# Half-width gated pairs: the norm's factor of the up branch is applied behind the lower projection, and VectorE takes the gate product in PSUM

## The chip, the cores and the metric

The kernel runs on one core of a Trainium2 chip. TensorE (PE) does the matrix products; a product needs a weight load (PEld) and a pass of the moving operand, and writes an accumulator bank of PSUM. VectorE (DVE), ScalarE (ACT) and GpSimd (POOL) do elementwise work; DVE and ACT read and write PSUM and SBUF, while the program uses GpSimd on SBUF tiles alone. Transfers from DRAM are issued by SyncE (SP). Each engine works through its own queue in order; engines wait for one another on semaphores. The metric is the device time of one execution in microseconds, the median of several.

## The reference, cut to what matters

Two layers over 512 tokens of 1024 channels, in float32. Layer 0 is a causal convolution module and a gated feed-forward network; layer 1 is windowed attention and another feed-forward network. The parts that the change touches are the first feed-forward network and its norm:

```python
def rmsnorm(x, g):
    xf = x * lax.rsqrt(jnp.mean(x * x, axis=-1, keepdims=True) + EPS)
    return xf * g

def swiglu_ffn(x, w_up, w_down):
    gate, up = jnp.split(x @ w_up, 2, axis=-1)
    return (jax.nn.silu(gate) * up) @ w_down

h = h + swiglu_ffn(rmsnorm(h, norm_ffn[l]), ffn_w_up[l], ffn_w_down[l])
```

The hidden width is 2816. The norm's factor, rsqrt of the mean square, is one number per token. It passes through a product with a weight matrix, so gate and up can be computed from the unscaled activations and scaled afterwards. In the up branch, which enters linearly, it can also pass through the lower projection; in the gate branch it cannot, because silu is not linear.

## The kernel before, in words

**Layout.** Channels lie on the 128 partitions, tokens along the free dimension. The stream `h` is 8 tiles of 128 channels by 512 tokens. A float32 product is made of three products in a faster format: each operand is split into a rounded part and a rest (`hi`, `lo`), and `mm3` (L254 to L256) adds hi*hi, hi*lo and lo*hi into one bank.

**Weights.** They come as 200-odd chunks of 128 x 1024 in the order of a list (`PLAN`). SyncE loads them up to six chunks ahead (L186). Up to two chunks ahead, ACT casts a chunk to its rounded part (L202, tile `whi`) and DVE subtracts it for the rest (L203, tile `wlo`). Three buffers of each exist, so the cast of a chunk waits until TensorE is done with the chunk three before it.

**Stages.** The convolution's input projection and the first token half's convolution come first. Then, for the first token half (256 tokens): the convolution's output projection (`pw2`, L694) and six of the eleven column pairs of the first feed-forward network (`ffn_part(0, 0, ..)`). The second token half's convolution runs as background work beside that, its steps handed out as TensorE uses up weight chunks. After it `pw2` and the same six pairs for the second token half follow, then the other five pairs for all 512 tokens at once, then layer 1.

**The convolution beside it.** Of the 31 taps of a channel tile, 18 (8 in the first two tiles) go over ACT, which scales a shifted row (L576), and GpSimd, which adds it up (L577). The others are taken by DVE with a multiply and add in PSUM (L584). At the end GpSimd adds both sums (L587); in the first four tiles DVE adds a shift (L611); ACT squares the row (L613); and TensorE sums row and square over channels (L622).

**A half-width pair.** A pair is 256 gate columns and 256 up columns. TensorE makes them in two banks, one for gate and one for up, out of four weight chunks of 24 matmuls each (`ffn_up`). `evac` then works on whole banks (128 x 512, two column tiles by 256 tokens): DVE multiplies gate by the norm's factor into a temporary (L433), ACT takes silu of it (L436), DVE multiplies up by the factor into another temporary (L433 again), GpSimd multiplies both (L437), and `split` makes the rounded part on ACT (L371) and the rest on DVE (L372), the tiles `quad` that the lower projection reads. The first pair's evac is held back until the second pair's second chunk, because the norm's factor is not known earlier.

**The lower projection.** `ffn_part` runs it in two groups of 512 output channels (`down_group`), each with two banks of two output tiles. Behind each group DVE adds the four tiles to `h`, one 128 x 256 tile at a time (L418).

**What orders the work.** The program is built with a scheduler that lays the instructions of each queue in the order of a simulated timeline (`schedule_with_timeline_sim=True`); the order is fixed then. PSUM is a pool of eight banks, and a tile takes whichever slot is free in that timeline. In the background the convolution holds up to four of them. The full-width pairs (512 tokens) have their own branch of `evac` (L441 to L446) and are not edited.

Of the kernel before, what the change touches and what calls it, by code (L numbers as in the profile page):

```python
# [12 lines left out]
AF = mybir.ActivationFunctionType  # L13
# [4 lines left out]
P = 128  # L18
# [130 lines left out]
def hybrid_trunk(ctx: ExitStack, tc: tile.TileContext, xT, W, prm_in, wdw_in, sinks, relb, onehot, outT):  # L149
    nc = tc.nc  # L150
# [10 lines left out]
    def uid(s):  # L161
        ctr[0] += 1
        return f"{s}{ctr[0]}"

    def bank():
        return ps.tile([P, 512], F32, tag="bank", name=uid("bank"))
# [4 lines left out]
    def temp():  # L171
        return tmp.tile([P, 512], F32, tag="tmp", name=uid("tmp"))

    def f32(ap):
        return ap.bitcast(F32)
# [95 lines left out]
    hT = cpool.tile([P, KT, S], F32, tag="h", name="h")  # L271
# [98 lines left out]
    def split(dst, src):  # L370
        nc.scalar.copy(dst[0], src)  # L371
        nc.vector.tensor_sub(dst[1], src, f32(dst[0]))  # L372

    def cut(pair, tok):
        return pair[0][:, tok], pair[1][:, tok]


    def accs(w):
        if w == 512:
            return [bank() for _ in range(4)]  # L380
        return [b[:, e * w:(e + 1) * w] for b in (bank(), bank()) for e in range(2)]

    def opens(m, w):
        return w == 512 or m % 2 == 0

    def closes(m, w):
        return w == 512 or m % 2 == 1


    def down_group(keys, act_of, banks, on_step=None):  # L390
        nk = len(keys)
        w = banks[0].shape[-1]
        for ci, (key, kts) in enumerate(keys):
            whi, wlo = get(*key)
            order = [(k, m) for k in range(2) for m in range(4)]
            if ci == nk - 1:
                order = [(k, m) for m in range(4) for k in range(2)]
            for k, m in order:
                sl = slice(m * P, (m + 1) * P)
                mm3(banks[m], (whi[:, k, sl], wlo and wlo[:, k, sl]), act_of(kts + k),  # L400
                    ci == 0 and k == 0 and opens(m, w), ci == nk - 1 and k == 1 and closes(m, w))
                if on_step is not None and ci < nk - 1 and m == 3:
                    on_step()
            if on_step is not None and ci == nk - 1:
                on_step()
                on_step()

    def ffn_part(layer, part, xg, tok, rms, on_h=None):
        lo, hi = (HALVES0, HALVES1)[layer][part]
        hid = ffn_up(layer, lo, hi, xg, tok, rms)  # L410
        w = tok.stop - tok.start
        for g in range(2):
            banks = accs(w)
            down_group([(("down", layer, kp, g), 2 * (kp - lo)) for kp in range(lo, hi)],
                       lambda kt: hid[kt], banks)
            for m in range(4):
                t = h[g * 4 + m][:, tok]
                nc.vector.tensor_add(t, banks[m], t)  # L418
                if on_h is not None:
                    on_h(g * 4 + m)  # L420

    def ffn_up(layer, lo, hi, xg, tok, rms):
        w = tok.stop - tok.start
        hid = Act(2 * (hi - lo), w)

        def evac(pair, banks):
            rs_bc = rms.step2()
            if w == 256:
                i = 2 * (pair - lo)
                dst = [q[:, i % 8:i % 8 + 2, :].rearrange("p a s -> p (a s)") for q in hid.q[i // 8]]  # L430
                t1, t2 = temp(), temp()
                for t, b in ((t1, banks[0]), (t2, banks[1])):
                    nc.vector.tensor_mul(t.rearrange("p (a s) -> p a s", a=2), b.rearrange("p (a s) -> p a s", a=2),  # L433
                                         rs_bc.unsqueeze(1).to_broadcast([P, 2, w]))
                    if t is t1:
                        nc.scalar.activation(t, t, AF.Silu)  # L436
                nc.gpsimd.tensor_mul(t2, t1, t2)  # L437
                split(dst, t2)
                return
            for m in range(2):  # L440
                t1, t2 = temp()[:, 0:w], temp()[:, 0:w]  # L441
                nc.vector.tensor_mul(t1, banks[m], rs_bc)  # L442
                nc.scalar.activation(t1, t1, AF.Silu)  # L443
                nc.vector.tensor_mul(t2, banks[2 + m], rs_bc)  # L444
                nc.gpsimd.tensor_mul(t2, t1, t2)  # L445
                split(hid[2 * (pair - lo) + m], t2)  # L446

        pending = []
        for pair in range(lo, hi):
            if w == 256:  # L450
                full = [bank(), bank()]
                banks = [b[:, e * w:(e + 1) * w] for b in full for e in range(2)]
            else:
                full = banks = accs(w)
            for half in range(2):
                for which in range(2):
                    whi, wlo = get("up", layer, pair, half, which)
                    order = [(k, m) for k in range(4) for m in range(2)]
                    if half == 1:
                        order = [(k, m) for m in range(2) for k in range(4)]  # L460
                    for k, m in order:
                        sl = slice(m * P, (m + 1) * P)
                        mm3(banks[which * 2 + m], (whi[:, k, sl], wlo[:, k, sl]), cut(xg[half * 4 + k], tok),
                            half == 0 and k == 0 and opens(m, w), half == 1 and k == 3 and closes(m, w))
                    if half == 0 and which == 1:
                        if w == 512:
                            rms.step1()
                        for p in pending:
                            evac(*p)
                        pending = []  # L470
            if w == 256 and pair == lo:
                rms.step1()
                pending.append((pair, full))
            else:
                evac(pair, full)
        return hid

    class Next:
# [5 lines left out]
        def on_h(self, i):  # L484
            if self.x is None:
                self.x = {self.gains[0]: Act(KT)}
            if self.rms is None:
                self.bc = new_bc() if self.bc is None else self.bc
                self.rms = Rms(self.bc, self.tok)
            g = self.gains[0]  # L490
            split_scaled(cut(self.x[g][i], self.tok), h[i][:, self.tok], col(g, i))
            self.rms.add(h[i][:, self.tok])
# [302 lines left out]
    if True:  # L795
        ffn_part(0, 1, x0["ffn0"], ALL, Both(), nxt.on_h)
        x, rms = nxt.x, nxt.rms
# [18 lines left out]
        for half in range(2):  # L816
# [7 lines left out]
            if half == 0:  # L824
                rs_bc = rms.step2()
                rs = rms.rs
                for m in range(2):
                    t = temp()
# [4 lines left out]
        for n in range(4):  # L833
            t = temp()
# [86 lines left out]
        banks = [bank() for _ in range(4)]  # L921
# [3 lines left out]
        banks = [bank() for _ in range(4)]  # L925
# [6 lines left out]
        for part in range(2):  # L932
            for g in range(2):
                banks = [bank() for _ in range(4)]
# [3 lines left out]
                for m in range(4):  # L938
                    i = g * 4 + m
# [153 lines left out]
```

## Time and profile before

| | us |
|---|---|
| median of the runs | 1135.75 (1135.62 to 1136.22) |
| the profiled execution | 1136.61, its span 1134.8 |
| TensorE busy | 1104.5 |
| DVE busy | 666.1 |
| ACT busy | 513.3 |
| GpSimd busy | 341.4 |
| first half-width pass of the feed-forward network, about | 180 to 290 |
| second half-width pass, about | 305 to 420 |

In a row of the timeline stand the start, the duration, the engine, the line of the kernel, the operation, the tiles written and read with their shapes, and in brackets the idle time before it with what ended it. In a group of instructions the numbers behind the bar are busy us in all, the mean of one in ns, and the idle time before them with its main enders. The table by stretch gives for each stretch the busy time of each engine with its count of instructions. Rows that follow each other on one engine may be merged, with a count behind them. A TensorE row's end is modelled, so rows of matmuls overlap; their starts tell the pace.

### The profile page before, as it was taken

To read this page: it belongs to the slowest core of one execution; us is meant where nothing else is said; L and a number is where in the kernel's file an instruction comes from. 1 tells how busy PE (TensorE), PEld (TensorE's weight loads), DVE (VectorE), ACT (ScalarE), POOL (GpSimd) and SP (SyncE) were. 2 spreads that over 40 slices of the span, in tenths; PEclk is the share of its full clock that TensorE was granted. 3 is DMA by queue.
4 is the path that set the end of the run, shared out by engine and by line. 5 is a ranking of instruction groups with operands and counts; after the bars stand their busy time and mean duration, and the time that the engine had idled before them with its cause. 6 is when DMAs were issued, how large, how long until landed. Compare 5 with 4: busy or idle time off the path is not lost.

```text
span 1134.8 us, 16051 instructions
## 1 busy us (share of the span) xinstructions
PE 1104.5 (97%) x6126; PEld 961.7 (85%) x6126; DVE 666.1 (59%) x1071; ACT 513.3 (45%) x898; POOL 341.4 (30%) x437
## 2 busy tenths in 40 slices
PE   6999999899999999999999999999999999999997
PEld 5888789899999998888878778888888888888886
DVE  3998748897876643454464675764454333444455
ACT  2786887744654432232352574653332222222234
POOL 2997989921011001121220242332111100110014
PEclk9999999999999999999999999999999999999998
DMA  9380044456555552223323211113323332233232
GB/s 358 112 95 1 0 149 149 130 188 237 171 188 184 186 186 93 93 93 108 96 75 106 81 38 38 38 56 109 96 93 94 102 101 93 93 99 104 95 97 89
DMA packets 41577, 128.16 MB, mean 113 GB/s; under 512 B 4475, under 2 KB 12828, under 8 KB 41500
## 3 DMA queue, kind: packets, MB, share of 16 engines
q1 hardware_dynamic: 40924, 126.69, 35.9%
q8 instruction: 48, 0.79, 0.3%
q10 hardware_dynamic: 576, 0.44, 0.1%
q14 instruction: 29, 0.24, 0.1%
HBM read 121.87 MB, written 5.24 MB: 112 GB/s over the span
## 4 chain that ended last, share of the span: by engine, by line
PE 84%; POOL 5%; DVE 4%; issue 3%; ACT 3%; DMA 0%; SPq 0%; POOLq 0%; ACTq 0%; DVEq 0%
PE bank L254 24%; PE bank L255 24%; PE bank L256 24%; PE bank L535 8%; POOL pr L577 3%; PE bank L864 1%; DVE wlo L203 1%; DVE quad L368 1%; PE bank L885 1%; ACT whi L202 1%; ACT pr L576 1%; PE bank L622 1%; DVE bank L584 1%; DMA h<-in_xT_dram 0%; ACT z L662 0%
## 5 line engine op out<-in xcount | busy, mean ns | idle before, releaser
L255 PE MATMUL bank<-quad,whi 128*128 128x512 f32 (+1 forms) x1584 | 543.4, 343 | 2.0 <-DVE quad L368 2.0
L256 PE MATMUL bank<-quad,wlo 128*128 128x512 f32 (+1 forms) x1584 | 542.4, 343 | 2.4 <-DVE wlo L203 2.4
L254 PE MATMUL bank<-quad,whi 128*128 128x512 f32 (+1 forms) x1584 | 543.0, 344 | 0.2
L203 DVE TENSOR_TENSOR wlo<-raw,whi 128x1024 fp32r<-128x1024 f32 x200 | 272.6, 1363 | 316.8 <-ACT whi L202 306.2
L202 ACT CAST whi<-raw 128x1024 fp32r<-128x1024 f32 x200 | 209.3, 1048 | 338.4 <-PE bank L255 295.8
L255 PEld LDWEIGHTS bank<-quad,whi 128*128 128x128 f32 x1584 | 300.7, 190 | 37.6 <-DVE quad L368 2.7
L256 PEld LDWEIGHTS bank<-quad,wlo 128*128 128x128 f32 x1584 | 300.2, 190 | 38.1 <-DVE wlo L203 3.4
L254 PEld LDWEIGHTS bank<-quad,whi 128*128 128x128 f32 x1584 | 300.4, 190 | 36.5 <-ACT quad L903 0.6
L445 POOL TENSOR_TENSOR tmp<-tmp,tmp 128x512 f32<-128x512 f32 x32 | 45.6, 1426 | 426.7 <-DVE tmp L444 412.2
L577 POOL TENSOR_TENSOR pr<-pr,pr 128x256 f32<-128x256 f32 x208 | 158.6, 798 | 7.5 <-ACT pr L576 6.5
L535 PE MATMUL bank<-quad,w 128*128 128x256 f32 x512 | 116.4, 388 | 8.4 <-DMA w<-in_W_dram 8.4
L535 PEld LDWEIGHTS bank<-quad,w 128*128 128x128 f32 x512 | 99.2, 195 | 23.3 <-DVE quad L510 8.3
L576 ACT ACTIVATE pr<-apad,wdw 128x256 f32<-128x256 f32 x208 | 102.1, 504 | 36.4 <-POOL pr L577 27.6
L584 DVE SCALAR_TENSOR_TENSOR bank<-apad,wdw,bank 128x256 f32<-128x256 f32 x248 | 114.7, 485 | 4.1
L325 POOL TENSOR_TENSOR tmp<-tmp,tmp 128x256 f32<-128x256 f32 (+1 forms) x42 | 44.8, 1066 | 121.9 <-ACT tmp L321 100.5
L443 ACT ACTIVATE tmp<-tmp 128x512 f32<-128x512 f32 x32 | 20.1, 632 | 86.4 <-DVE tmp L442 86.4
L878 POOL TENSOR_SCALAR sc<-sc,sm 128x256 f32<-128x256 f32 (+1 forms) x64 | 30.8, 503 | 86.1 <-DVE sm L876 86.0
L371 ACT CAST quad<-tmp 128x512 fp32r<-128x512 f32 (+1 forms) x60 | 35.3, 592 | 43.5 <-POOL tmp L445 25.8
L372 DVE TENSOR_TENSOR quad<-tmp,quad 128x512 fp32r<-128x512 f32 (+1 forms) x60 | 40.0, 671 | 3.2 <-ACT quad L371 3.2
L437 POOL TENSOR_TENSOR tmp<-tmp,tmp 128x512 f32<-128x512 f32 x12 | 19.7, 1644 | 72.1 <-DVE tmp L433 55.5
L368 DVE SCALAR_TENSOR_TENSOR quad<-h,prm,quad 128x512 fp32r<-128x512 f32 (+1 forms) x40 | 39.4, 1017 | 2.2 <-ACT quad L367 2.0
L444 DVE TENSOR_TENSOR tmp<-bank,rsbc 128x512 f32<-128x512 f32 x32 | 22.1, 691 | 30.4 <-PE bank L256 30.4
(129 smaller groups left out, 754.2 us busy)
## 6 DMA issues: line engine op xcount, KB each, us to landing
raw<-in_W_dram SPq DMA_DIRECT2D x208, 512.0 KB, 3.6
w<-in_W_dram SPq DMA_DIRECT2D x16, 512.0 KB, 9.4
fd<-fs SPq DMA_DIRECT2D x1, 3072.0 KB, 33.8
h<-in_xT_dram SPq DMA_DIRECT2D x8, 256.0 KB, 6.4
bias<-fd SPq DMA_DIRECT2D x8, 256.0 KB, 6.3
out_dram<-res SPq DMA_DIRECT2D x13, 128.0 KB, 1.8
out_dram<-res ACTq DMA_DIRECT2D x3, 128.0 KB, 2.4
wdw<-in_wdw_dram SPq DMA_DIRECT2D x1, 124.0 KB, 6.1
```

Of the source, the lines that this page charges most:

```text
L202: nc.scalar.copy(hi, r)
L203: lo_engine[0].tensor_sub(lo, r, f32(hi))
L254: nc.tensor.matmul(out, w[0], x[0], start=start, stop=False)
L255: nc.tensor.matmul(out, w[0], x[1], start=False, stop=False)
L256: nc.tensor.matmul(out, w[1], x[0], start=False, stop=stop)
L325: self.eng.tensor_add(sq, self.acc, sq)
L368: nc.vector.scalar_tensor_tensor(dst[1], src, g, f32(dst[0]), op0=ALU.mult, op1=ALU.subtract)
L445: nc.gpsimd.tensor_mul(t2, t1, t2)
L535: mm = nc.tensor.matmul(self.pb[:, w * W2:(w + 1) * W2], w1[ct][:, w, k, :], x[k] if x else xg[k][:, tok], start=k == 0, stop=k == KT - 1)
L576: on_act = nc.scalar.mul(pr, a[:, j:j + W2], tap(j))
L577: nc.gpsimd.tensor_add(pr, acc, pr)
L584: on_dve = nc.vector.scalar_tensor_tensor(yt if i == nd - 1 else c, src, tap(i), c if i else self.shift, op0=ALU.mult, op1=ALU.add)
```

## The change

At half width, three things are different. The up bank is no longer scaled: after silu of the scaled gate, DVE multiplies the up bank by it in place, in PSUM, and `split` reads that bank. GpSimd has no part in it. The lower projection then yields sums that lack one factor of the norm; behind each group DVE multiplies each bank by the factor in place (both output tiles at once) and adds it to two tiles of `h` with one instruction. The banks of the lower projection are the same two as before, now also named as a whole (`full`). The full-width pairs stay as they are.

```diff
@@ ffn_part
         for g in range(2):
-            banks = accs(w)
+            if w == 256:
+                full = [bank().rearrange("p (a s) -> p a s", a=2) for _ in range(2)]
+                banks = [b[:, e, :] for b in full for e in range(2)]
+            else:
+                banks = accs(w)
             down_group([(("down", layer, kp, g), 2 * (kp - lo)) for kp in range(lo, hi)],
                        lambda kt: hid[kt], banks)
+            if w == 256:
+                rs_bc = rms.step2().unsqueeze(1).to_broadcast([P, 2, w])
+                for e, b in enumerate(full):
+                    i = g * 4 + 2 * e
+                    nc.vector.tensor_mul(b, b, rs_bc)
+                    nc.vector.tensor_add(hT[:, i:i + 2, tok], b, hT[:, i:i + 2, tok])
+                    for k in range(2 if on_h is not None else 0):
+                        on_h(i + k)
+                continue
             for m in range(4):
...
@@ evac in ffn_up, w == 256
-                t1, t2 = temp(), temp()
-                for t, b in ((t1, banks[0]), (t2, banks[1])):
-                    nc.vector.tensor_mul(t.rearrange("p (a s) -> p a s", a=2), b.rearrange("p (a s) -> p a s", a=2),
-                                         rs_bc.unsqueeze(1).to_broadcast([P, 2, w]))
-                    if t is t1:
-                        nc.scalar.activation(t, t, AF.Silu)
-                nc.gpsimd.tensor_mul(t2, t1, t2)
-                split(dst, t2)
+                t1 = temp()
+                nc.vector.tensor_mul(t1.rearrange("p (a s) -> p a s", a=2), banks[0].rearrange("p (a s) -> p a s", a=2),
+                                     rs_bc.unsqueeze(1).to_broadcast([P, 2, w]))
+                nc.scalar.activation(t1, t1, AF.Silu)
+                nc.vector.tensor_mul(banks[1], banks[1], t1)
+                split(dst, banks[1])
                 return
```

## The prediction

> **What bounds the kernel now.** I read the page's engine totals first, then the busy table by stretch for the part of the span that the change touches, then what TensorE waited for there.
>
> ```profile
> span 1134.8 us, 16051 instructions
> PE 1104.5 (97%) x6126; PEld 961.7 (85%) x6126; DVE 666.1 (59%) x1071; ACT 513.3 (45%) x898; POOL 341.4 (30%) x437
> ```
>
> TensorE (PE) is the bound as a whole, and the change takes no matmul away: time can only come from or go into TensorE's waits. The half-width passes, where the edited branches run, lie between about 180 and 420 us. The next rows are the busy table (stretch, length, then busy us and count of PE, PEld, DVE, ACT and POOL, then the clock and the DMA's share).
>
> ```profile
> 180.00:200.00 20.00, 20.00 (x165) 19.86 (x164) 15.47 (x25) 14.33 (x27) 18.37 (x22) 1.00 0.44 137
> 200.00:210.00 10.00, 7.51 (x59) 6.90 (x57) 8.09 (x12) 7.13 (x13) 9.49 (x8) 1.00 0.49 150
> 210.00:220.00 10.00, 9.35 (x69) 8.94 (x70) 8.28 (x14) 7.97 (x16) 9.92 (x12) 1.00 0.37 127
> 220.00:230.00 10.00, 8.81 (x73) 8.60 (x72) 8.74 (x13) 5.84 (x9) 7.79 (x8) 1.00 0.43 141
> 230.00:260.00 30.00, 29.83 (x241) 29.25 (x240) 29.00 (x49) 14.31 (x18) 8.09 (x5) 1.00 0.60 191
> 260.00:300.00 40.00, 40.00 (x325) 39.31 (x324) 31.83 (x59) 22.75 (x36) 3.44 (x5) 1.00 0.64 221
> 300.00:420.00 120.00, 120.00 (x1001) 119.95 (x1000) 78.48 (x84) 56.09 (x73) 15.59 (x14) 1.00 0.57 182
> ```
>
> TensorE is full from 230 us on, so the second half-width pass (300 to 420) has nothing to win. What there is to win lies between 200 and 230, where GpSimd (POOL) is busy without a break. The timeline of TensorE there has these waits (in brackets: idle before, and who ended it):
>
> ```profile
> 202.31 0.39 PE L256 MATMUL bank<-quad,wlo 128*128 128x256 f32 x1 [0.59 <-DVE wlo L203]
> 205.94 0.39 PE L256 MATMUL bank<-quad,wlo 128*128 128x256 f32 x1 [0.49 <-DVE wlo L203]
> 210.35 0.70 PE L622 MATMUL bank<-y,ones_m 128*128 128x256 f32 x2 [1.77 <-DVE y L611]
> 212.78 0.70 PE L622 MATMUL bank<-sq,ones_m 128*128 128x256 f32 x2 [0.30 <-ACT sq L613]
> 223.25 0.39 PE L256 MATMUL bank<-quad,wlo 128*128 128x256 f32 x1 [1.19 <-DVE wlo L203]
> ```
>
> Together 0.59 + 0.49 + 1.77 + 0.30 + 1.19 = 4.34 us: the most that can go. The longest is the sum over channels of the convolution's second token half (L622), which waits for y (L611), which waits for GpSimd's last addition (L587). GpSimd's own timeline says why that is late:
>
> ```profile
> 201.18 1.67 POOL L577 TENSOR_TENSOR pr<-pr,pr 128x256 f32<-128x256 f32 x1 [0.51 <-DVE tmp L433]
> 202.81 1.30 POOL L437 TENSOR_TENSOR tmp<-tmp,tmp 128x512 f32<-128x512 f32 x1
> 204.06 2.41 POOL L577 TENSOR_TENSOR pr<-pr,pr 128x256 f32<-128x256 f32 x2
> 206.43 1.75 POOL L437 TENSOR_TENSOR tmp<-tmp,tmp 128x512 f32<-128x512 f32 x1
> 208.14 2.39 POOL L587 TENSOR_TENSOR y<-y,pr 128x256 f32<-128x256 f32 x2
> 210.49 11.63 POOL L577 TENSOR_TENSOR pr<-pr,pr 128x256 f32<-128x256 f32 x13
> ```
>
> Two gate products (L437) stand in GpSimd's queue among the convolution's tap additions (L577) and ahead of L587.
>
> **The change part by part.** *GpSimd's product goes.* Twelve L437 leave its queue, six per pass:
>
> ```profile
> L437 POOL TENSOR_TENSOR tmp<-tmp,tmp 128x512 f32<-128x512 f32 x12 | 19.7, 1644 | 72.1 <-DVE tmp L433 55.5 <-ACT tmp L436 11.1 <-DVE bank L584 3.0
> L433 DVE TENSOR_TENSOR tmp<-bank,rsbc 128x512 f32<-128x512 f32 x24 | 16.2, 684 | 5.4 <-PE bank L256 5.4
> L372 DVE TENSOR_TENSOR quad<-tmp,quad 128x512 fp32r<-128x512 f32 x12 | 9.0, 752 | 0.9 <-ACT quad L371 0.9
> L418 DVE TENSOR_TENSOR h<-bank,h 128x256 f32<-128x256 f32 x16 | 6.0, 417 | 0.5 <-PE bank L256 0.4
> L889 DVE TENSOR_TENSOR ptl<-bank,pth 128x512 fp32r<-128x512 f32 x28 | 18.9, 687 | 6.2 <-ACT pth L888 6.0
> L548 DVE TENSOR_TENSOR bank<-bank,rsbc 128x256 f32<-128x256 f32 x2 | 0.9, 432 | 0.1
> ```
>
> That frees 12 x 1.644 = 19.7 us of GpSimd. What of it counts is the first pass, while GpSimd is the late one.
>
> *DVE (VectorE).* Per pair of column tiles it had two scalings (L433) and the residual's subtraction (L372); it then has one scaling, one product in PSUM and the subtraction, so the count stays. A product that writes PSUM is shown only at 256 elements (L548, 432 ns, beside 417 for L418 into SBUF), so I take 0.69 us for 512 elements; with L433's 684 as the lower bound and 15 ns more as the upper, 12 of them differ by under 0.2 us. The subtraction reading PSUM is L889's shape, 687 instead of 752 ns: 12 x 0.065 = 0.8 us less. Behind each of the four lower groups, four additions of 417 ns (1.67 us) become two scalings and two additions at 0.69 (2.76 us): 4 x 1.09 = 4.4 us more. Sum: about +3.6 us on DVE, none of it at a place where TensorE waits now.
>
> *The cover of those 1.09 us.* What could be late behind them is the next weight split (L203):
>
> ```profile
> 400.85 1.23 DVE L203 TENSOR_TENSOR wlo<-raw,whi 128x1024 fp32r<-128x1024 f32 x1 [1.65 <-ACT whi L202]
> 402.00 1.53 DVE L418 TENSOR_TENSOR h<-bank,h 128x256 f32<-128x256 f32 x4
> 403.74 1.23 DVE L203 TENSOR_TENSOR wlo<-raw,whi 128x1024 fp32r<-128x1024 f32 x1 [0.20 <-ACT whi L202]
> ```
>
> A split takes 1.23 us of a period of 2.88 us (403.74 less 400.85) and DVE otherwise idles 1.65 us before it; a split moved by about 1.0 us is still ready within its period, and the splits are made a chunk ahead. I cost it at nothing. Were the cover gone it would cost at most 4 x 1.09 = 4.4 us. In the first pass's lower groups DVE is fuller (31.83 of 40 us), but 8 us stay free for 2.2 us of added work.
>
> *PSUM.* The second bank of each pair is held until the subtraction has read it. In the built order the next pairs' first matmuls wait for a bank only at the second chunk of the third pair, for the gate bank of the first, which the first scaling frees as before. No cost.
>
> *What moves.* The build orders every queue by a simulated timeline, so the edit reshuffles queues, but only in the half-width passes. Three of these moves matter, all in the first pass: L587 directly follows the tap additions; the channel sum L622 stands 16 matmuls earlier on TensorE; and on ScalarE (ACT) two more tap products (L576) stand ahead of the weight cast that serves the wait at 223.25. SyncE's queue swaps one weight load with one bias load (273 to 279 us, where no TensorE wait is).
>
> *The sum, by hand from the rows.* First, y. In the rows GpSimd is free at 202.85 (201.18 + 1.67). Two tap additions at the 0.89 us that 11.63 / 13 gives, then L587's pair at its own 2.39, end at 202.85 + 1.79 + 2.39 = 207.0 instead of 210.5: 3.5 us earlier. In DVE's rows
>
> ```profile
> 204.37 1.52 DVE L203 TENSOR_TENSOR wlo<-raw,whi 128x1024 fp32r<-128x1024 f32 x1 [0.34 <-ACT whi L202]
> 209.88 0.42 DVE L611 TENSOR_TENSOR y<-y,bank 128x256 f32<-128x256 f32 x1 [0.61 <-POOL y L587]
> ```
>
> the first L611 so starts at 209.88 - 3.5 = 206.4, and the sum could start at 206.85 instead of 210.35. TensorE, after the wait at 205.94 (which stays, since its cast on ScalarE waits for the addition that ends at 202.85), reaches the moved sum four matmuls later, about 206.4. So 1.77 becomes about 0.4: 1.4 us gained. One scaling less stands ahead of the split behind 202.31: 0.2 us more. The squares' wait of 0.30 stays.
>
> Second, the wait at 223.25. It ends with the split that follows this cast:
>
> ```profile
> 220.06 0.51 ACT L576 ACTIVATE pr<-apad,wdw 128x256 f32<-128x256 f32 x1 [0.30 <-POOL pr L577]
> 220.47 1.03 ACT L202 CAST whi<-raw 128x1024 fp32r<-128x1024 f32 x1
> ```
>
> The product ahead of the cast waits for the tenth of the 13 additions; in the new order it is the twelfth. GpSimd is 3.5 us ahead, less 2 x 0.89: the cast comes 1.7 us earlier. TensorE arrives 1.6 us earlier. So this wait stays about as it is, and it sets the total: 1.6 to 1.7 us. From 224 us on TensorE has no wait to lose and DVE has no more work per chunk than before.
>
> I take 1.6 us. The profiled execution took 1136.61 us around its span of 1134.8; 0.86 above the median of 1135.75. Span 1133.2, median 1135.75 - 1.6 = 1134.15, written 1134.2. Its own range is 1133.0 to 1135.2. What a measurement can tell from no change is 0.2%, 2.3 us, so the likeliest outcome is "same".
>
> **The rivals.** *Given back at the fourth pair.* Every gain of 201 to 215 must pass the cast at 220.47. If the two products moved ahead of it cost their full GpSimd time with contention (1.2 us each, as in 2.41 / 2) and the silu ahead of it waits too, it comes no earlier, and the time is 1135.7 +- 0.7. For: 223.25 is a wait on the same queue. Against: GpSimd's lead of 3.5 us is larger than 2.4.
>
> A variant has the clock in it. These rows show the granted clock (last but two) in three 3 us stretches:
>
> ```profile
> 172.00:175.00 3.00, 1.32 (x7) 0.98 (x6) 3.00 (x7) 2.46 (x7) 3.00 (x4) 0.91 1.00 385
> 175.00:178.00 3.00, 3.00 (x16) 2.91 (x15) 2.96 (x7) 3.00 (x9) 3.00 (x5) 0.53 0.18 74
> 208.00:211.00 3.00, 1.23 (x8) 0.98 (x8) 2.38 (x4) 1.57 (x4) 3.00 (x4) 1.00 0.48 186
> ```
>
> ```profile
> PE bank L255 <- DVE quad L368: 1.2, 1, 1.2
> ```
>
> After 1.68 us of idling in 3 us (172 to 175; the table of waits has its longest, 1.2 us) the clock fell to about a half. Then 16 matmuls ran in 3 us, where 180 to 200 holds 165 in 20, which is 24.75 in 3 us and 0.12 us each: (24.75 - 16) x 0.12 = 1.1 us lost. After 1.77 us (208 to 211) it did not fall. A wait of over 2 us at the cast would put it at even odds; then 0.5 us of the gain are left. The Trainium skill ("TensorE: Matmul & The Clock Gate", section "Why this matters for your kernels") asks only that no idle gap exceed about 3 us; by it no wait here would lower the clock and the sum would stand. The trace does not agree: the fall at 175 followed gaps of which the longest is 1.2 us, so the measurement decides and I keep the case.
>
> *All waits go.* If splits and casts run ahead once GpSimd is quick, all but the 0.49 and 0.30 go: 0.59 + 1.77 + 1.19 = 3.6 us, up to 4.34: 1131.4 to 1132.2. For: 19.7 us of GpSimd time leave, and splits without GpSimd beside them take 1.21 us (237.06) instead of 1.66 (216.26). Against: ScalarE's queue still stands behind the tap additions.
>
> ```profile
> 216.26 1.66 DVE L203 TENSOR_TENSOR wlo<-raw,whi 128x1024 fp32r<-128x1024 f32 x1 [1.42 <-ACT whi L202]
> 237.06 1.21 DVE L203 TENSOR_TENSOR wlo<-raw,whi 128x1024 fp32r<-128x1024 f32 x1
> ```
>
> *The sum is asked too early (slower).* The new order has TensorE ask for y 16 matmuls, 1.9 us, earlier. That pays only if GpSimd really comes forward. If L587 ended where it ends now, TensorE would idle from 206.4 to 210.35, 3.95 us instead of 1.77, and the clock would fall (1.1 us): 1135.75 + 2.2 + 1.1 = 1139.0. It turns from gain to loss where y comes less than 1.9 us earlier, against the 3.5 worked out. The two new products in DVE's queue, which wait for ScalarE's silu, are the way it could come about.
>
> **How the numbers follow.** The likeliest case 0.45; given back or halved by the clock 0.20; all waits go 0.18; asked too early 0.17. The range is 1131.3 (the far end of "all go", less 0.1) to 1137.8, midway in the slower case. Faster by over 0.2% (below 1133.5): 0.18 and the low tail of the likeliest, 0.27. Slower (above 1138.0): 0.15. Same: 0.58.
>
> **What would show it.** Right: no L437 row; L587 after the second pair ending near 207 us; the wait at L622 under 1 us; one wait of 1 to 2 us left before a split near 221; no new TensorE waits after 225; DVE up by about 3.6 us. Wrong: a wait of 3 us or more at the channel sum, a half clock near 207 or 222, or waits in the lower groups (255 to 295 or 400 to 420).

## The result, and the profile after

| | median (us) | lowest to highest | runs |
|---|---|---|---|
| before | 1135.75 | 1135.12 to 1136.42 | 7 |
| after | 1132.64 | 1132.16 to 1133.85 | 7 |

The changed kernel takes 0.9971 of the time before, with a 95% interval of 0.9962 to 0.9980: 3.1 us less by the medians, 2.3 to 4.3 by the interval. That is beyond the 0.2% (2.3 us) that the prediction took as the border of "same", with one end of the interval on the border itself; by that border the outcome is "faster". One execution of product_into_sbuf, a run below, took 1376.3 us with a mean granted clock of 0.753 and is left out of its time. The profiled execution took 1132.94 us around a span of 1131.2. In after the lines of the kernel stand twelve further down: the tap additions L577 are L589, the last addition L587 is L599, y (L611) is L623, the channel sum L622 is L634. The splits (L203) and casts (L202) keep their numbers.

The page's engine totals after the change:

```profile
span 1131.2 us, 16049 instructions
PE 1103.4 (98%) x6126; PEld 961.2 (85%) x6126; DVE 664.0 (59%) x1071; ACT 512.3 (45%) x898; POOL 321.8 (28%) x425
```

GpSimd lost 19.6 us, as worked out (12 x 1.644). VectorE lost 2.1 us where +3.6 was forecast. The busy table by stretch, with the columns explained in the prediction:

```profile
200.00:210.00 10.00, 8.98 (x67) 8.37 (x65) 9.56 (x16) 9.80 (x20) 9.49 (x11) 1.00 0.46 143
210.00:220.00 10.00, 9.54 (x76) 9.05 (x74) 8.31 (x12) 7.74 (x15) 10.00 (x12) 1.00 0.50 158
220.00:230.00 10.00, 9.25 (x77) 9.25 (x78) 9.96 (x17) 5.18 (x7) 1.29 (x1) 1.00 0.61 190
230.00:260.00 30.00, 30.00 (x247) 29.79 (x246) 28.98 (x48) 13.01 (x17) 2.41 (x2) 1.00 0.61 183
260.00:300.00 40.00, 40.00 (x325) 39.31 (x324) 31.10 (x54) 22.76 (x36) 3.44 (x5) 1.00 0.69 221
```

Read it by counts. From 200 to 300 us TensorE now runs 67 + 76 + 77 + 247 + 325 = 792 matmuls; before it ran 59 + 69 + 73 + 241 + 325 = 767. The 25 more, at the 0.12 us of a matmul, are 3.0 us: the whole gain lies in these 100 us. GpSimd, busy until 228 us before, is done at 221. The waits of TensorE that are left in this stretch, from its timeline:

```profile
201.89 0.39 PE L256 MATMUL bank<-quad,wlo 128*128 128x256 f32 x1 [0.38 <-DVE wlo L203]
205.67 0.38 PE L256 MATMUL bank<-quad,wlo 128*128 128x256 f32 x1 [0.64 <-DVE wlo L203]
206.25 0.59 PE L634 MATMUL bank<-y,ones_m 128*128 128x256 f32 x2
208.71 0.59 PE L634 MATMUL bank<-sq,ones_m 128*128 128x256 f32 x2
220.75 0.39 PE L256 MATMUL bank<-quad,wlo 128*128 128x256 f32 x1 [1.19 <-DVE wlo L203]
```

They sum to 2.21 us instead of 4.34. Both waits at the channel sum, 1.77 for y and 0.30 for its squares, are gone; the wait of 1.19 is there to the hundredth, only 2.50 us earlier (220.75 instead of 223.25). GpSimd's timeline shows the cause:

```profile
200.96 2.87 POOL L589 TENSOR_TENSOR pr<-pr,pr 128x256 f32<-128x256 f32 x3 [0.51 <-ACT pr L588]
203.78 2.42 POOL L599 TENSOR_TENSOR y<-y,pr 128x256 f32<-128x256 f32 x2
206.16 15.12 POOL L589 TENSOR_TENSOR pr<-pr,pr 128x256 f32<-128x256 f32 x16
```

No product stands among the additions, and the pair of last additions ends at 206.2 us instead of 210.5. The cast and the split that end the wait of 1.19 come 2.50 us earlier too, each on its own engine's timeline (before: the cast at 220.47):

```profile
217.97 1.03 ACT L202 CAST whi<-raw 128x1024 fp32r<-128x1024 f32 x1
219.04 1.66 DVE L203 TENSOR_TENSOR wlo<-raw,whi 128x1024 fp32r<-128x1024 f32 x1 [0.89 <-ACT whi L202]
```

The first product behind the convolution's last sum dates the gain. Before, then after:

```profile
273.28 0.95 PE L630 MATMUL bank<-ident,tmp 128*128 128x1 f32 x8
```

```profile
270.08 0.95 PE L642 MATMUL bank<-ident,tmp 128*128 128x1 f32 x8
```

So the kernel is 2.50 us ahead at 221 and 3.20 at 270. Of both, 0.20 us stood already at the wait near 173 us (it ends at 173.24 before and at 173.04 after), ahead of anything that the change touches: 2.30 and 3.00 us are the change's.

### The profile page after: what moved, and what is told of

It is laid out like the page before. It is cut to its first block, busy times and chain, and to the rows that moved or that the text cites. A ratio compares the mean times of both kernels' runs of the same rounds, so it can differ in the third digit from the quotient of the medians.

```text
span 1131.2 us, 16049 instructions
## 1 busy us (share of the span) xinstructions
PE 1103.4 (98%) x6126; PEld 961.2 (85%) x6126; DVE 664.0 (59%) x1071; ACT 512.3 (45%) x898; POOL 321.8 (28%) x425
## 4 chain that ended last, share of the span: by engine, by line
PE 79%; POOL 5%; DVE 5%; issue 4%; ACT 4%; DMA 2%; SPq 0%; POOLq 0%; ACTq 0%; DVEq 0%
PE bank L254 25%; PE bank L255 25%; PE bank L256 25%; POOL pr L589 4%; PE bank L876 1%; ACT pr L588 1%; DVE bank L596 1%; PE bank L252 1%; DVE quad L368 1%; DVE wlo L203 1%; DMA w<-in_W_dram 1%; ACT whi L202 1%; PE bank L897 1%; DMA lhs<-in_relb_dram 1%; DMA h<-in_xT_dram 1%
## 5 line engine op out<-in xcount | busy, mean ns | idle before, releaser
L203 DVE TENSOR_TENSOR wlo<-raw,whi 128x1024 fp32r<-128x1024 f32 x200 | 267.3, 1337 | 313.9 <-ACT whi L202 304.0
L202 ACT CAST whi<-raw 128x1024 fp32r<-128x1024 f32 x200 | 209.6, 1048 | 354.1 <-PE bank L255 305.0
L457 POOL TENSOR_TENSOR tmp<-tmp,tmp 128x512 f32<-128x512 f32 x32 | 45.6, 1427 | 485.0 <-DVE tmp L456 471.5
L589 POOL TENSOR_TENSOR pr<-pr,pr 128x256 f32<-128x256 f32 x208 | 157.1, 786 | 7.4 <-ACT pr L588 7.0
L371 ACT CAST quad<-tmp 128x512 fp32r<-128x512 f32 (+1 forms) x48 | 27.9, 585 | 29.6 <-POOL tmp L457 25.7
L886 ACT ACTIVATE sc<-sc,m 128x257 f32<-128x257 f32 (+1 forms) x64 | 30.2, 475 | 15.2 <-DVE m L879 15.0
L372 DVE TENSOR_TENSOR quad<-tmp,quad 128x512 fp32r<-128x512 f32 (+1 forms) x48 | 31.0, 651 | 2.3 <-ACT quad L371 2.3
```

The costliest lines, as they stand in the source:

```text
L202: nc.scalar.copy(hi, r)
L203: lo_engine[0].tensor_sub(lo, r, f32(hi))
L589: nc.gpsimd.tensor_add(pr, acc, pr)
```

## The experiments

All times are medians; each ratio is against the kernel before, run on the same chip in the same session, with its 95% interval.

| run | time (us) | ratio | interval |
|---|---|---|---|
| first_pass_only | 1132.87 | 0.9972 | 0.9961 to 0.9983 |
| second_pass_only | 1135.48 | 0.9995 | 0.9987 to 1.0004 |
| late_factor_gpsimd_product | 1135.98 | 0.9998 | 0.9989 to 1.0007 |
| early_factor_dve_product | 1140.81 | 1.0040 | 1.0028 to 1.0053 |
| extra_scaling_first_pass | 1134.81 | 0.9991 | 0.9982 to 0.9999 |
| idle_gpsimd_product | 1133.59 | 0.9980 | 0.9971 to 0.9989 |
| cover_lower_groups | 1132.96 | 0.9973 | 0.9962 to 0.9983 |
| product_into_sbuf | 1133.30 | 0.9979 | 0.9969 to 0.9989 |
| twelve_tap_buffers | 1133.86 | 0.9982 | 0.9974 to 0.9991 |
| sixteen_tap_buffers | 1136.86 | 1.0012 | 1.0003 to 1.0021 |
| tap_moved_pair1 | 1133.24 | 0.9977 | 0.9968 to 0.9986 |
| tap_moved_pair1_pair3 | 1131.06 | 0.9959 | 0.9947 to 0.9972 |

The kernel before had medians of 1136.07, 1135.88 and 1135.77 in the three sessions (four rows each).

A second yardstick comes from the profiled executions: the time from the end of the wait near 173 us, ahead of the edited code, to the first product behind the convolution's last sum (L630 before, L642 after).

| run | from the wait near 173 to that product (us) |
|---|---|
| before | 100.04 |
| after | 97.04 |
| first_pass_only | 97.09 |
| second_pass_only | 100.05 |
| late_factor_gpsimd_product | 100.05 |
| early_factor_dve_product | 103.35 |
| extra_scaling_first_pass | 99.08 |
| idle_gpsimd_product | 97.93 |
| cover_lower_groups | 97.03 |
| product_into_sbuf | 98.04 |

### Where: the first pass or the second

```diff
@@ ffn_part
-            if w == 256:
+            late = w == 256 and tok == HALF[0]
+            if late:
...
-            if w == 256:
+            if late:
...
@@ evac
+                if tok == HALF[0]:
...
+                else:
...
```

Behind `if` stands the changed code, behind `else` the code of before. The second run has HALF[1] in place of HALF[0].

> The edit stands in the first half-width pass alone; the second has the code of before. Theory (the whole gain comes from GpSimd's queue between 200 and 224 us): as fast as the changed kernel, 1132.3 to 1133.3 us, a gain of 2.5 to 3.4 on the 1135.75 of before, with the channel sum near 206 without a wait and the wait of 1.2 us before a split near 221 still there. Rival (the second pass and its lower groups give part of it): 1133.8 to 1134.8.

> The edit stands in the second half-width pass alone. Theory: no change, 1135.2 to 1136.2 us, since TensorE has no wait between 300 and 420 us to lose; GpSimd's and VectorE's totals move and nothing else does. Rival (the second pass gives part of the 3.1 us): 1134.8 or less.

Both came out as the theory had them. The first pass alone gives 0.9972, the whole gain; the second alone gives nothing that can be measured (0.9995, 1 inside the interval), though it takes as many products from GpSimd.

### What: the product's engine or the factor's place

The change is two edits, and each can be made without the other. With the factor late and the product left on GpSimd, VectorE has a copy where the scaling was:

```diff
-                nc.vector.tensor_mul(banks[1], banks[1], t1)
-                split(dst, banks[1])
+                t2 = temp()
+                nc.vector.tensor_copy(t2, banks[1])
+                nc.gpsimd.tensor_mul(t2, t1, t2)
+                split(dst, t2)
```

> The factor stands behind the lower projection as in the changed kernel, but the gate product is given back to GpSimd: VectorE copies the second half out of PSUM where before it scaled it. So the scalings are moved and GpSimd's queue is that of before. Theory (GpSimd's queue is the cause): no gain, 1135.2 to 1136.3 us, the channel sum waits 1.5 to 2.0 us near 210. Rival (where the factor is applied, and the shorter chain to the product, give the gain): 1132.5 to 1134.0. If the 4 x 1.09 us more on VectorE behind the lower groups cost anything, it shows here as a time above 1136.5.

With the factor early and the product on VectorE, one word of the kernel before is changed:

```diff
-                nc.gpsimd.tensor_mul(t2, t1, t2)
+                nc.vector.tensor_mul(t2, t1, t2)
```

> Before, with one word changed: the half-width gate product is taken by VectorE out of SBUF, both scalings and the factor stay where they were. VectorE so has 12 products of about 0.7 us more and GpSimd 12 fewer. Theory (GpSimd's queue is the cause): most of the gain, 1132.6 to 1134.2 us, a little less than the changed kernel because 4 us more of VectorE work stand between 190 and 260 us, where it is 80 to 97% busy. Rival (VectorE can take the product only because a scaling is given up): 1135.8 to 1138, with waits for weight splits between 220 and 260.

| | product on GpSimd | product on VectorE |
|---|---|---|
| factor ahead of the product | 1 (before) | 1.0040 |
| factor behind the lower projection | 0.9998 | 0.9971 (after) |

Moving the factor alone does nothing, and the channel sum waits its 1.77 us as before. Moving the product alone loses 4.7 us. Here the theory was wrong; the rival had the direction, but the time lies above its range, and the largest waits are not for weight splits between 220 and 260 but for the channel sums behind 270. Only both together gain. The reason for the loss stands in VectorE's timeline of the early-factor run: the fourth pair's last taps

```profile
271.42 0.86 DVE L584 SCALAR_TENSOR_TENSOR y<-apad,wdw,bank 128x256 f32<-128x256 f32 x2
```

came at 271.42; in the kernel before the same row stands at 266.83, and after the change at 262.56. TensorE, asking for the last channel sums, waits:

```profile
272.81 0.70 PE L622 MATMUL bank<-y,ones_m 128*128 128x256 f32 x2 [2.38 <-POOL y L587]
274.48 0.70 PE L622 MATMUL bank<-y,ones_m 128*128 128x256 f32 x2 [0.52 <-POOL y L587]
276.30 1.05 PE L630 MATMUL bank<-ident,tmp 128*128 128x1 f32 x8 [0.68 <-ACT tmp L627]
```

These 3.58 us are a new place of waiting: neither before nor after has a wait there.

### Is it the added work on VectorE?

```diff
+                if tok == HALF[0]:
+                    nc.vector.tensor_scalar(banks[1], banks[1], 1.0, None, op0=ALU.mult)
                 nc.vector.tensor_mul(banks[1], banks[1], t1)
```

> The changed kernel with one VectorE instruction more per pair in the first half-width pass: a multiplication of the second bank by 1.0, 128x512 in PSUM, ahead of the product. So VectorE has the scaling back that the change spares it, 6 x 0.69 = 4.1 us, and GpSimd stays free of products. Theory (in the run with the early factor and VectorE's product it was these 4.1 us that made the fourth pair's last taps late, to 271 us, with TensorE waiting for the last channel sums): slower than before, 1136.5 to 1141 us, with waits at the channel sum near 270. Rival (that run lost by the product's two sources in SBUF, beside GpSimd): 1132.5 to 1134.5.

At 1134.81 us it lies between the two ranges, above the rival's and below the theory's: 2.2 us of the 3.1 are lost, but it is not slower than before. The wait near 220 (219.78 here) ends 47.72 us behind the one near 173, as after the change (47.71; before 50.01). So what GpSimd's queue gave is all there, and the loss comes behind it. In TensorE's timeline the new place of waiting is there again, smaller (the lines stand two further down than in after):

```profile
268.23 0.70 PE L636 MATMUL bank<-y,ones_m 128*128 128x256 f32 x2 [0.66 <-POOL y L601]
271.14 1.05 PE L644 MATMUL bank<-ident,tmp 128*128 128x1 f32 x8 [0.68 <-ACT tmp L641]
```

VectorE's total is 3.4 us above that of the changed kernel (667.4 against 664.0), a little under the 4.1 expected, and they cost 2.2 us: the spared scaling is a condition of most of the gain. The early-factor run lost 6 us more than this one. Its product out of two SBUF operands averaged 787 ns instead of 693 and took 1.22 us in one place beside GpSimd; its first-pass waits at 206.48 (1.30 for a cast) and 212.06 (0.83 for the squares) are not in this run either. In the two profiled executions (1139.36 and 1135.38 us) TensorE's waits between 185 and 277 us differ by 4.1 us: 2.24 at the last sums and 1.85 between 200 and 223. What makes the engines that late there, and the other 2 us between the medians, the runs do not settle.

### Is it how busy GpSimd is?

```diff
+                if tok == HALF[0]:
+                    nc.gpsimd.tensor_mul(temp(), t1, t1)
                 split(dst, banks[1])
```

> The changed kernel with a GpSimd product per pair in the first half-width pass whose result nobody reads (128x512, the form of before). Only GpSimd's queue is filled as before; no data depends on it. Theory (the gain is GpSimd's queue): most of the gain goes, 1134.3 to 1136 us, the channel sum near 207 to 210 waits again by 1 us or more. Rival (the gain is the shorter chain from the gate's banks to the hidden activation): 1132.4 to 1133.4.

The theory's forecast was missed: 1133.59 us keeps 2.3 of the 3.1 us, 0.2 above the rival's range. GpSimd's timeline tells why y is not late:

```profile
201.79 1.04 POOL L451 TENSOR_TENSOR tmp<-tmp 128x512 f32<-128x512 f32 x1
202.79 2.41 POOL L591 TENSOR_TENSOR pr<-pr,pr 128x256 f32<-128x256 f32 x2
205.16 1.42 POOL L601 TENSOR_TENSOR y<-y,pr 128x256 f32<-128x256 f32 x2
207.23 1.04 POOL L451 TENSOR_TENSOR tmp<-tmp 128x512 f32<-128x512 f32 x1
```

Nobody waits for these products, and the built order has the second one behind y. One product ahead of y, 1.04 us long, leaves y ready at 206.6 and the channel sum waiting 0.17 us. The wait at 220.33 ends 47.71 us behind the one near 173, as after the change, so up to there nothing is lost. The 0.9 us come behind it, with a wait that the changed kernel has not:

```profile
224.10 0.39 PE L256 MATMUL bank<-quad,wlo 128*128 128x256 f32 x1 [0.64 <-DVE wlo L203]
```

The cast for that split stands on ScalarE behind a tap product that waited 1.04 us (220.90) for GpSimd's additions, which stand behind the third idle product (218.15). So this run did not put the products where they stood before, and it does not test two products ahead of y; it shows that 9.2 us more of GpSimd work in all cost 0.95 us. The rival, a shorter chain to the hidden activation, has this against it: neither before nor after does TensorE wait for a hidden activation between 180 and 300 us.

### The cover behind the lower groups, and PSUM

```diff
                     nc.vector.tensor_mul(b, b, rs_bc)
+                    for _ in range(2):
+                        nc.vector.tensor_scalar(b, b, 1.0, None, op0=ALU.mult)
```

> The changed kernel with two multiplications by 1.0 more behind each of the two banks of the four lower groups of the half-width passes: 4 x 4 x 0.69 = 11 us more on VectorE, 5.5 of them in each pass. Theory (VectorE has the room there): no change against the changed kernel, 1132.4 to 1133.6 us. Rival (in the first pass the 5.5 us push the fourth pair's taps and the rows behind them, as VectorE's 4.1 us did between 190 and 260): 1134 to 1138 us, with waits near 270 to 295.

At 1132.96 us this is the changed kernel's time. VectorE's work in the first pass's lower groups rose from 31.10 to 34.37 us of 40, and TensorE's row did not move:

```profile
260.00:300.00 40.00, 40.00 (x325) 39.31 (x325) 34.37 (x60) 23.07 (x36) 3.44 (x5) 1.00 0.70 214
```

The place of the work decides: VectorE work is free here (8.5 us more in its total) and costs two thirds of its length (2.2 of 3.4) in the pairs ahead of these groups.

```diff
-                nc.vector.tensor_mul(banks[1], banks[1], t1)
-                split(dst, banks[1])
+                t2 = temp()
+                nc.vector.tensor_mul(t2, banks[1], t1)
+                split(dst, t2)
```

> The changed kernel with VectorE's product written to a temporary in SBUF instead of back into its PSUM bank; ScalarE's cast and the subtraction then read SBUF. Theory (that the product is VectorE's and the scaling is spared is what counts, not where it is written): as the changed kernel, 1132.3 to 1133.6 us; the subtraction back at about 0.75 instead of 0.69 us, 12 x 0.06 us hidden. Rival (writing and reading PSUM, away from GpSimd, is part of the gain): 1134 to 1135.5 us.

1133.30 us lies inside the theory's range, and the interval overlaps that of the changed kernel. The profiled execution, the slowest of the nine (1134.28), has a wait of 0.97 us at the channel sum (206.06) that the changed kernel has not, and its yardstick is 1.00 us longer. At most about 1 us of the gain so belongs to PSUM as the destination; whether any does, the runs do not settle.

### What the remaining waits are

```diff
-pr = cv.tile([P, W2], F32, tag="pr", name=uid("pr"), bufs=8)
+pr = cv.tile([P, W2], F32, tag="pr", name=uid("pr"), bufs=12)
```

> The changed kernel with 12 buffers for the tap products (pr) instead of 8. What is left between 200 and 224 us are three waits for weight splits, 0.38 + 0.64 + 1.19 = 2.2 us; ahead of each, ScalarE's cast stands behind tap products that wait for a GpSimd addition. Theory (they wait for one of the 8 buffers to come free): with 12, part or all of the 2.2 us goes, 1130.4 to 1132.2 us. Rival (GpSimd's rate decides, whatever ScalarE has ahead of it, or the reordered queues only move the wait): 1132.3 to 1133.5.

> The same with 16 buffers. Theory (buffers): no slower than with 12, 1130.2 to 1132 us. Rival (no use beyond what GpSimd can add): as the changed kernel, 1132.3 to 1133.5, with the wait of about 1.2 us near 221 still there.

The three waits did hang on the buffers, as the theory had it, but the time, 1133.86 us, lies above both ranges: the wait only moved, as the rival had it. With 12 buffers the three weight waits of 2.21 us are all gone; only 0.31 us is left between 200 and 300, at the channel sum. But TensorE and GpSimd show what came in their place, the norm of the second token half:

```profile
193.82 0.70 PE L360 MATMUL bank<-tmp,ones_m 128*128 128x256 f32 x2 [2.27 <-ACT tmp L347]
```

```profile
183.13 9.25 POOL L589 TENSOR_TENSOR pr<-pr,pr 128x256 f32<-128x256 f32 x9
192.34 0.70 POOL L339 TENSOR_TENSOR rs<-ms,mhalf 128x2 f32<-128x2 f32 x1
```

With more buffers ScalarE runs ahead, more tap additions stand in GpSimd's queue ahead of the norm's inverse root (L339), and TensorE waits for that. With 16 buffers the norm's sum of squares is late, by 6 us:

```profile
190.88 1.02 PE L335 MATMUL bank<-ones_c,tmp 128*128 128x1 f32 x4 [6.06 <-POOL tmp L325]
```

That run is slower than before (1.0012), outside both ranges. Of the three counts the kernel's 8 has the lowest time, though its interval overlaps that of 12.

```diff
-N_POOL = ((13, 13, 12, 12), (8, 18, 18, 18))
+N_POOL = ((13, 13, 12, 12), (8, 17, 18, 19))
```

The first of the next two runs has (8, 17, 18, 18).

> The changed kernel with one tap of each column tile of the second pair moved from ScalarE and GpSimd to VectorE in the convolution of the second token half (8, 17, 18, 18). GpSimd's queue is 2 x 0.89 us shorter and ScalarE's 2 x 0.5, VectorE's 2 x 0.48 longer. Theory (the waits left are GpSimd's and ScalarE's): 1131.2 to 1132.3 us. Rival (VectorE, 97% busy from 230 to 260 us, makes the fourth pair late): 1133 to 1135.

> The same, and one tap of each column tile of the fourth pair moved the other way (8, 17, 18, 19), so that every engine has as many taps as in the changed kernel and only when they come due differs. Theory (GpSimd is late up to 221 us and idle behind it, VectorE the other way round): 1131 to 1132.3 us. Rival (the fourth pair's additions on GpSimd stand in the same stretch up to 221, so nothing is freed): 1132.4 to 1134.

The first gives 1133.24 us, in the rival's range and no gain over the changed kernel: its weight waits fall to 0.37 and 0.83, but waits of 0.74 at the squares and 1.06 at L642 (269.74) come in. At L642 its profiled execution is still 0.19 us ahead by the yardstick (96.85); it lost 1.6 us behind it, where TensorE's clock was halved (see the last section). The second gives 1131.06 us, the fastest here; its five runs lie between 1131.00 and 1131.53, below all seven of the changed kernel. That is in the range of the theory, but not for its reason. TensorE's timeline has the same kind of waits between 200 and 224:

```profile
184.13 0.39 PE L256 MATMUL bank<-quad,wlo 128*128 128x256 f32 x1 [0.42 <-DVE wlo L203]
203.53 0.39 PE L256 MATMUL bank<-quad,wlo 128*128 128x256 f32 x1 [0.37 <-DVE wlo L203]
209.39 0.70 PE L634 MATMUL bank<-sq,ones_m 128*128 128x256 f32 x2 [0.75 <-ACT sq L625]
218.60 0.39 PE L256 MATMUL bank<-quad,wlo 128*128 128x256 f32 x1 [0.58 <-DVE wlo L203]
```

The product L360 stands at 190.01 instead of 191.88 and L642 at 268.13 instead of 270.08: 1.87 of the 1.95 us are won by 190 us, and 1.37 of them between the wait near 173 and there (17.47 us instead of 18.84): the clock stayed full, and the wait for a split that takes 1.05 us elsewhere in such a case (see the last section) is 0.42. Why the moved taps do this is not shown.

## Why the prediction was right, and where its sizes were off

The forecast was 1134.2 us, "same", with a range of 1131.3 to 1137.8; 1132.64 lies in the range, 0.4 us below the likeliest case's own 1133.0. The range holds it because it was drawn to take in the rival of "all waits go", so the hit owes something to its width; the gain of 3.1 us is nearly twice the 1.6 forecast, and "faster" had a chance of 0.27 where "same" had 0.58. The mechanism it was built on, GpSimd's two products leaving the queue ahead of y, is what the runs show for the 2.3 us won by 221; the 0.7 behind it have another cause. Step by step:

- *GpSimd's 19.7 us go; only the first pass counts.* Right: 19.6 us, and the second pass alone gives nothing.
- *y ends at 207.0 instead of 210.5, the wait of 1.77 falls to about 0.4.* Mis-sized, the first of the terms that failed. The pair ended at 206.2: three additions took 2.87 us from 200.96, where I had 1.67 + 1.79 from 201.18. TensorE reached the sum at 206.25 and did not wait at all: 1.77 gained, not 1.4.
- *The squares' wait of 0.30 stays.* Wrong. The squares are made of the same y and came 4.60 us earlier on ScalarE (207.72 instead of 212.32), while TensorE takes them 4.07 us earlier (208.71 instead of 212.78): the wait went with y's.
- *0.2 at the first split, 0.49 stays.* Right within 0.15 (0.59 became 0.38; 0.49 became 0.64).
- *The wait of 1.19 stays, because cast and TensorE come forward alike.* Right to the hundredth, but both came 2.50 us forward (2.30 without the 0.20 of 173 us) and not 1.7 and 1.6: GpSimd was 4.3 us ahead behind y, not 3.5, and 4.3 less two additions of 0.945 (15.12 / 16) is 2.4.
- *The terms together.* 1.77 + 0.30 + 0.21 - 0.15 = 2.13 us of waits went, where I had 1.6.
- *Nothing to win from 224 us on.* Wrong by 0.7 us (3.20 at 270 against 2.50 at 221): a term put at nothing. TensorE's row for 230 to 260 had 29.83 of 30 busy, and I took it for full; it now runs 247 matmuls there instead of 241. A short wait hardly shows in a modelled busy time, but it shows in the starts. Before, TensorE comes to the matmuls at 235.03 and 238.33 in 0.24 and 0.45 us, where 0.12 is the pace, and to the next one in 0.22 each time; with 0.06 at 226.40 that is 0.71 us over the pace. After the change no such gap stands between 221 and 270, the channel sums aside. Before:

```profile
232.60 1.29 POOL L437 TENSOR_TENSOR tmp<-tmp,tmp 128x512 f32<-128x512 f32 x1 [4.73 <-DVE tmp L433]
233.16 1.81 DVE L203 TENSOR_TENSOR wlo<-raw,whi 128x1024 fp32r<-128x1024 f32 x1
235.03 0.38 PE L256 MATMUL bank<-quad,wlo 128*128 128x256 f32 x1
238.33 0.39 PE L256 MATMUL bank<-quad,wlo 128*128 128x256 f32 x1 [0.17 <-DVE wlo L203]
```

  Beside GpSimd's product a weight split took 1.81 us and ended at 234.97; the next one stands behind it in VectorE's full queue (237.06 to 238.27). The two runs that have that product as before (second pass alone; late factor with GpSimd's product) show the same split at 1.81 us and the same wait of 0.17; with the edit in the first pass alone it takes 1.22 us and no wait is there. So nearly all of these 0.7 us came from a split that GpSimd no longer slows, and not from its queue.
- *VectorE +3.6 us, hidden.* By its own rows the edit added 4.3 us: 8.2 + 8.2 + 8.2 + 5.6 + 5.3 = 35.5 us (the remaining scaling and the four last rows below), where 16.2 + 9.0 + 6.0 = 31.2 stood. But the splits got 5.3 us shorter, and 1.1 us went in small amounts elsewhere. Behind each lower group 1.22 us came in, not 1.09: the four additions took 1.50 us together (6.0 / 4), where I had 4 x 0.417. The group rows, before and then after:

```profile
L203 DVE TENSOR_TENSOR wlo<-raw,whi 128x1024 fp32r<-128x1024 f32 x200 | 272.6, 1363 | 316.8 <-ACT whi L202 306.2 <-PE bank L360 4.2 <-PE bank L864 3.9
```

```profile
L203 DVE TENSOR_TENSOR wlo<-raw,whi 128x1024 fp32r<-128x1024 f32 x200 | 267.3, 1337 | 313.9 <-ACT whi L202 304.0 <-PE bank L360 4.2 <-PE bank L876 3.9
L449 DVE TENSOR_TENSOR bank<-bank,tmp 128x512 f32<-128x512 f32 x12 | 8.2, 695 | 3.4 <-PE bank L256 3.4
L372 DVE TENSOR_TENSOR quad<-bank,quad 128x512 fp32r<-128x512 f32 x12 | 8.2, 683 | 0.0
L425 DVE TENSOR_TENSOR bank<-bank,rsbc 128x512 f32<-128x512 f32 x8 | 5.6, 696 | 0.9 <-PE bank L256 0.7
L426 DVE TENSOR_TENSOR h<-bank,h 128x512 f32<-128x512 f32 x8 | 5.3, 683 | 0.0
```

  The prices of the single operations were right: 695 ns for the product in PSUM (0.69 taken), 683 for the subtraction (687), 696 and 683 for the scaling and addition (690). What I left out is that GpSimd's products had slowed the splits beside them. The kernel with the edit in the first pass alone, whose second pass still has GpSimd's products, averages 1326 ns for a split between 300 and 420 us, the changed kernel 1223. That agrees with the Trainium skill ("SBUF — State Buffer", section "Who interferes with whom"), by which a VectorE instruction with two SBUF inputs contends with a GpSimd instruction that reads SBUF. Of the 5.3 us, 4.4 lie in the second pass, where nothing waits, and bought no time; 0.6 are the one split of the first pass shown above, and bought the 0.7.
- *The 1.09 us behind each lower group cost nothing.* Right, and another 8.5 us cost nothing either.
- *PSUM: no cost.* Right: no wait of TensorE that the profile names between 180 and 300 us is for a bank.
- *Given back at the fourth pair, or by the clock.* It did not come. The cast is 2.50 us earlier, and the clock is 1.00 from 208 to 226 us.
- *The slower rival.* Its trigger, VectorE's product standing late, did not come with this edit; but the early-factor run lost 4.7 us, and not at the sum near 206 where the rival put it: the loss that stands out is at the fourth pair's sums near 270. I had written that the count of VectorE instructions per pair stays as a remark; it was the condition of the gain.
- *All waits go* gave 1131.4 to 1132.2. The time came near it, 0.4 above, but the mechanism did not: 2.21 us of waits stayed.

## What to carry to other kernels

Moving an operation off a late engine pays where that engine's queue holds something the bounding engine waits for, and only there: the same edit gave everything in one pass and nothing in the other. Look for room on the receiving engine in that same stretch; here it came from algebra (a factor per token passes through the lower projection) and without it the move lost time. Where several waits hang on one late instruction, count them all as going with it, and ask what it releases behind it. Ask also which instructions it slows beside it: 0.7 of the 3.0 us came that way, in a stretch that read as full. And treat a buffer count as part of the queues' order, since four more buffers only moved the wait to the norm.

## What the runs showed of the hardware

The clock of TensorE fell to about a half after waits well under 3 us (the longest 1.06 us at one place, 1.77 at another), in some executions and not in others, with the same instructions and the same wait. In the kernel with the late factor and GpSimd's product the sum's wait of 1.77 us was followed by this (stretch table, clock last but two):

```profile
208.00:211.00 3.00, 1.23 (x8) 1.17 (x8) 2.38 (x5) 1.78 (x4) 3.00 (x3) 0.95 0.47 137
211.00:214.00 3.00, 3.00 (x14) 2.73 (x12) 2.77 (x5) 2.36 (x6) 3.00 (x4) 0.50 0.28 89
```

In the profiled execution of before, the same 1.77 us left the clock at 1.00, and so did a wait of 2.38 us in the early-factor run (1.00 from 272 to 281). In the run with the half clock the slower matmuls cost nothing in the end: the wait near 223, 1.19 us before, was 0.22, and it ends 50.02 us behind the wait near 173, against 50.01 before. The same holds for the half clock of 175 to 178 us. One stretch and a wait of the kernel with only the second pass edited, where the clock stayed full:

```profile
175.00:178.00 3.00, 3.00 (x23) 2.84 (x22) 2.89 (x7) 3.00 (x8) 3.00 (x5) 1.00 0.00 0
```

```profile
185.37 0.39 PE L256 MATMUL bank<-quad,wlo 128*128 128x256 f32 x1 [1.06 <-DVE wlo L203]
```

TensorE, not slowed, came early to a weight split and waited 1.06 us there; before and after have the half clock and no such wait. From the wait near 173 us to L360 it is 18.85 us in before, 18.84 in after and 18.87 in this run. In both places the half clock stood ahead of a wait for another engine and cost nothing.

Where no such wait follows, it did cost. In the first of the two runs with a moved tap:

```profile
269.74 1.05 PE L642 MATMUL bank<-ident,tmp 128*128 128x1 f32 x8 [1.06 <-ACT tmp L639]
```

```profile
272.00:275.00 3.00, 3.00 (x16) 3.00 (x16) 0.00 (x0) 0.74 (x3) 0.37 (x1) 0.50 1.01 271
```

From this product to the sum L360 near 330 us it is 61.37 us in this run, and 59.76 in before, in after and in the second run with moved taps: 1.6 us lost. The 1.1 us that the prediction charged for a half clock so depends on what follows. Ahead of the waits near 185 and 223 nothing was lost, and behind the last sum more than that.

The Trainium skill ("TensorE: Matmul & The Clock Gate", section "Part 1: The HAM clock gate (the "warmup" mystery)") says that the activity window runs free of the program, so that the point of change varies from run to run. The traces agree that it varies, though none shows the window itself: in the ten profiles whose instructions are the same up to there, the wait near 173 us ended at 172.91 to 173.25 in the five where the clock fell and at 172.06 to 172.95 in the five where it did not. Its figure of about 3.4 us of idling does not fit: the longest single wait there is about 1.3 us.
